# A two-layer decoder trunk: feed-forward chunk 11 as seven block products, row products in order of inner tiles, and convolution taps one slot behind their copy

## The chip, the cores and the metric

One core of a Trainium2 chip runs the whole program. The metric is the device time of one execution in microseconds (us). The engines are named as the profile names them: PE (TensorE, matmuls; PEld is its weight load), DVE (VectorE), ACT (ScalarE), POOL (GpSimd) and SP (SyncE, which issues DMAs).

## The reference

Two layers, a dilated windowed attention (layer 0) and a gated linear recurrence (layer 1), each followed by a gated convolutional feed-forward network (FFN), with a norm before and after each part. The change is in the FFN, which runs once in each layer, on 512 tokens of 1024 features:

```python
D_FF = 3 * D_MODEL           # 3072
def causal_dwconv(x, w, b):  # three taps along the tokens
    ...
    for k in range(K):
        out = out + xp[:, k:k + S] * w[k]
    return out
def conv_ffn(x, w_up, conv_w, conv_b, w_down):
    u = causal_dwconv(x @ w_up, conv_w, conv_b)
    g, v = u[..., :D_FF], u[..., D_FF:]
    return (jax.nn.gelu(g, approximate=True) * v) @ w_down
```

## The kernel before

Every float32 product is made of three matmuls on float32r operands (`mm3`, line 411): each operand is split into a rounded high part (made by ACT, line 150) and the rest (a subtraction on DVE, line 151, the "split" below), and high*high, high*low and low*high are summed in PSUM. PE runs one instruction stream, in the order in which the Python code issues it; so do DVE and ACT.

**The up projection.** D_FF is cut into 12 chunks j of 256 columns, once for the gate half g and once for the value half v. A chunk gives two inner tiles k = 2j and 2j+1 (128 features by 512 tokens). *Plain* chunks are computed tile by tile: 8 blocks of 128 input features, 3 matmuls each, so 24 matmuls 128x512 per tile (`feat_tile`, line 624; for j = 0 in two halves of 256 tokens, `feat_tiles(..., True)`). Before the change chunks 0, 1, 2 and 11 are plain, except for two value tiles of chunk 2 that serve as fillers. Chunks 3 to 10 (`SEVEN`) are computed as *seven block products*, Strassen's scheme on 2x2 blocks: per half and chunk seven products, 12 matmuls 128x256 each (`chain`, line 1006; matmuls at line 1019). Their weight sums are made in the raw weight tiles by two accumulating DMAs on POOL (line 187) and two adds on DVE (`across`, line 211, and `lower`, line 215). The token sums T that they need are built once per layer from hT by `token_sums` (line 914), a generator that runs piece by piece beside the tiles (one piece per tick) with 24 operations on DVE and 8 on ACT; its home is the buffer of the residual x, which a DMA on POOL (line 919) first saves to DRAM.

**Cycles and slots.** One chunk half is a *cycle* of ten slots (`CYCLE`). `AT` gives the slot of each of the seven products of a cycle: 1 in slot 0, 5 in slot 1, 2 in slot 2, 6 in slot 4, 3 in slot 5, 7 in slot 8, and 4 in slot 13, which is slot 3 of the next cycle. The free slots 6, 7 and 9 hold *fillers* of six matmuls 128x512: first eight quarters of the two value tiles of chunk 2, then the row products (down projection of finished inner tiles k, output columns 0 to 511, two token tiles at a time). A slot that is in no table is skipped: nothing is issued in it.

**What is issued behind a slot.** `slot` (line 366) first issues the matmuls of its step, then what `later(n, f)` put off until n slots on, then `tick`, which pumps at most one more split of a weight block for products to come. At most 16 split halves are alive, so a new split often waits until the slot that frees its buffer has ended.

**The two outputs of a cycle.** The upper output (bank y[0]) is finished by product 3: one slot later DVE adds a stored part to it (`upper`, line 1032), and `begin` runs the convolution: ACT copies the bank into u with scale and bias (line 774), then DVE adds the two shifted taps from PSUM (line 776, two instructions). The lower output (bank y[1]) first receives product 7; one slot behind product 7, DVE adds a stored part to its right half (line 1037), and product 4, on PE, accumulates onto it. So product 4 has to wait for the add of line 1037, and everything behind product 4 on PE waits with it. One slot after `begin`, `gate` multiplies g and v on DVE (line 793) or ACT applies the gelu (line 789).

After the seven-product part, `down` (line 837) runs the other half of the output columns and, for the inner tiles in `REST`, what is missing of the first.

Of the kernel before, what the change touches and what calls it, by code (L numbers as in the profile page):

```python
# [19 lines left out]
S = 512  # L20
# [15 lines left out]
TOE_BUFS = 2  # L36
CP_PAD = 8
WARM = 5
SEVEN = range(3, 11)
LAST, TAIL, REST = 11, 16, range(18, 22)  # L40
EARLIER = (0, 1, 2, 3, 22, 23, *range(4, 18))
AT = {1: 0, 5: 1, 2: 2, 6: 4, 3: 5, 7: 8, 4: 13}
CYCLE, FREE = 10, (6, 7, 9)
EARLY = 16
QUAD = {1: 0, 5: 2, 2: 3, 6: 4, 3: 6, 7: 8, 4: 12}
APART, ROUND = 7, 44
# [38 lines left out]
def kernel(  # L85
# [107 lines left out]
    def free_slots(n):  # L193

        end = CYCLE * n
        free = [CYCLE * c + r for c in range(n) for r in FREE][2:] + [end, end + 1]
        assert not {CYCLE * c + a for c in range(n) for a in AT.values()} & set(free)
        return free

# [158 lines left out]
    def side(steps, delay=1):  # L358
        sides.append([delay, steps])
# [3 lines left out]
    def later(n, f):  # L363
        due.append([n, f])
# [400 lines left out]
    def ffn(layer, hT, post, pre):  # L765
        ca, cc = ffn_cols[layer]
        neg = cp.tile([P, 144], F32, tag="neg", name=nm("neg"))
        nc.vector.tensor_scalar(neg[:, 0:96], ca, -1.0, None, op0=ALU.mult)
        nc.vector.tensor_scalar(neg[:, 96:144], cc[:, 0:48], -1.0, None, op0=ALU.mult)

        def conv(ps, j, minus=False):
            u = gen(s="u")
            near, far, own = (neg, neg, neg[:, 96:144]) if minus else (ca, ca, cc)
            nc.scalar.activation(u, ps, AF.Identity, scale=own[:, j : j + 1], bias=cc[:, 48 + j : 49 + j])  # L774
            for d, wc in ((1, near[:, 48 + j : 49 + j]), (2, far[:, j : j + 1])):
                nc.vector.scalar_tensor_tensor(  # L776
                    u[:, d:], ps[:, : S - d], wc, u[:, d:], op0=ALU.mult, op1=ALU.add
                )
            return u

        gv, ready = {}, set()

        def begin(b, ps, j, minus=False):
            m = b % 2
            k = 2 * j + m
            u = conv(ps, 24 * (b // 2) + k, minus)
            if b < 2:
                gv[k] = u
                return lambda: nc.scalar.activation(u, u, AF.Gelu_apprx_tanh)
            g = gv[k]  # L790

            def gate():
                nc.vector.tensor_tensor(g, g, u, op=ALU.mult)
                ready.add(k)

            return gate

        def tiles(j, i, bs):
            for b in bs:
                feat_tile(i, b % 2, hT, lambda ps: begin(b, ps, j))  # L800

        def gen_load(*srcs):
            o = []

            def load():
                for src in srcs:
                    o.append(gen(s="dw"))
                    nc.sync.dma_start(o[-1].rearrange("p (k c) -> p k c", c=src.shape[-1]), src)

            return o, load  # L810

        def act(k):
            assert k in ready, k
            return gv[k]

        direct = []
        for k in EARLIER:
            w = ffn_w_down[layer][k * P : (k + 1) * P, 0:512].rearrange("(k p) c -> p k c", p=P)
            o, load = gen_load(w)
            direct.append((("rows", k), load, lambda o=o: [o[0]], 0))  # L820
            direct.append((("act", k), None, lambda k=k: [act(k)], 2))
        up["direct"] = direct
        T = []
        for j in range(SEVEN[0] - 1):
            if j:
                side(token_sums(hT, T), 0)
                tiles(j, chunk(), (0, 1))
                tiles(j, chunk(), (2, 3))
            else:
                feat_tiles(2, hT, lambda b, ps: begin(b, ps, j)(), True)  # L830
        for j in (SEVEN[0] - 1, LAST):
            tiles(j, chunk(), (0, 1))
        tiles(LAST, chunk(), (2, 3))
        prep, run = down(act, post, pre)
        return run(seven(hT, T, begin, chunk(), lambda: prep(2)))

# [77 lines left out]
    def token_sums(hT, T, first=False):  # L914

        if not first:
            assert len(sides) == 1
            d = dp.tile([P, 4, D], F32, name=nm("x_kept"))
            nc.gpsimd.dma_start(d, X[0])
            kept.append(d)  # L920
# [122 lines left out]
    def seven(hT, T, begin, last, prep):  # L1043
# [2 lines left out]
        i0, acc, ends_at = state["next"], {}, CYCLE * 2 * len(SEVEN)  # L1046

        def finish(b, ps, j, minus=False):
            later(1, begin(b, ps, j, minus))

        def ends(j, half):
            return lambda ps: finish(2 * half, ps, j), lambda ps: finish(2 * half + 1, ps, j, True)
# [10 lines left out]
        fill = []  # L1063
        for m in range(2):
            fill += quarters(last, m, hT, lambda ps, m=m: finish(2 + m, ps, SEVEN[0] - 1))
        fill += [lambda k=k, p=p: rows(k, p) for k in EARLIER for p in ((0, 1), (2, 3))]
        steps = {}
        n = 0
        for j in SEVEN:
# [544 lines left out]
    for layer in range(2):  # L1614
        if layer:
# [5 lines left out]
                    w_cols(w_in, n * 256 + (D if kind == "b" else 0))  # L1621
            for c in range(4):
                w_rows(lru_w_out[0], c * 256)
        chunks = [(j, half) for j in range(SEVEN[0]) for half in range(2)]
        chunks[-1:] = [(LAST, 0), (LAST, 1), chunks[-1]]
        for j, half in chunks + [(j, half) for j in SEVEN for half in range(2)]:
            w_cols(ffn_w_up[layer], half * D_FF + j * 256, kind="seven" if j in SEVEN else "feat")
        for half, k in [(1, k) for k in range(0, TAIL, 4)] + [(0, REST[0])] + [(1, k) for k in range(TAIL, 24, 4)]:
            rows = ffn_w_down[layer][k * P : (k + 4) * P, half * 512 : half * 512 + 512]
# [86 lines left out]
```

## Time and profile before

| | |
|---|---|
| median of 3 runs | 1420.18 us (1419.66 to 1420.43) |
| the profiled execution | 1419.78 us, of which the span from first to last instruction 1418.0 us |
| PE busy | 1407.8 us (99% of the span), 8597 instructions |
| DVE busy | 1108.9 us (78%), 2173 instructions |
| ACT busy | 782.5 us (55%), 1622 instructions |
| FFN of layer 0 | up projection, plain part about 489 to 568 us, seven-product part about 568 to 794 us, then the down projection |
| FFN of layer 1 | the same from about 1029, 1108 and 1334 us |

A row of the timeline gives start, duration, engine, line, operation, output <- inputs, shapes and count, and in square brackets how long the engine had been idle before it and whose work ended that. Rows of one line that follow each other are merged (x2, x3): the duration is then that of the group. Matmuls overlap by their pipeline, so their spacing, not their duration, tells what one costs.

### The profile page before, as it was taken

Reading aid. Unit: us, or ns where it says so; the run is one execution under the profiler, and the core shown is the slowest. Engines: PE = TensorE matmul, PEld = TensorE weight load, DVE = VectorE, ACT = ScalarE, POOL = GpSimd, SP = SyncE. Lnnn points to the kernel's source line nnn. Section 1 sums busy time; section 2 is a strip of 40 time slices with the busy share of each in tenths; the row PEclk is TensorE's granted clock in tenths of the full one; section 3 lists DMA queues with packets and bytes.
Section 4 is the critical chain, followed back from the end, with each engine's and each line's share of the span. In section 5 each row is a group of like instructions: output and inputs, shape, how many; then the busy total and the mean of one; then the engine's idle time right before and its main releaser. Section 6 shows DMA issues by size and latency. Waiting matters only on the chain.

```text
span 1418.0 us, 23252 instructions
## 1 busy us (share of the span) xinstructions
PE 1407.8 (99%) x8597; PEld 1262.2 (89%) x8597; DVE 1108.9 (78%) x2173; ACT 782.5 (55%) x1622; POOL 215.3 (15%) x336
## 2 busy tenths in 40 slices
PE   9999999999999999999999999999999999999998
PEld 7888999999998898999999889888898999999886
DVE  6676898887866988988888758769788988888843
ACT  7343565353636554666656545589454655666641
POOL 0341332131310100212120001000101211111000
PEclk9999999999999999999999999999999999999999
DMA  7653464655665453756563632432444566665411
GB/s 227 180 144 111 120 181 152 173 160 164 172 189 187 153 178 82 171 120 164 120 156 84 221 119 90 134 119 73 136 149 112 120 139 144 154 130 127 167 57 59
DMA packets 167657, 199.79 MB, mean 141 GB/s; under 512 B 10432, under 2 KB 136856, under 8 KB 167288
## 3 DMA queue, kind: packets, MB, share of 16 engines
q1 hardware_dynamic: 123064, 153.34, 33.8%
q0 software_dynamic: 43632, 43.92, 16.6%
q8 instruction: 67, 1.10, 0.3%
q10 hardware_dynamic: 848, 1.05, 0.2%
q14 instruction: 46, 0.38, 0.1%
HBM read 179.31 MB, written 18.96 MB: 140 GB/s over the span
## 4 chain that ended last, share of the span: by engine, by line
PE 77%; DVE 4%; ACT 4%; issue 1%; DVEq 0%; ACTq 0%
PE ps L1019 31%; PE acc L413 25%; PE ps L413 13%; PE v L1212 6%; DVE wlo L151 1%; DVE xb L1517 1%; PE O L1424 1%; PE S L1358 1%; ACT whi L150 1%; ACT sig L1538 1%; PE tr L503 1%; ACT sig L1557 0%; ACT a L1555 0%; ACT xhi L150 0%; ACT th L1556 0%
## 5 line engine op out<-in xcount | busy, mean ns | idle before, releaser
L151 DVE TENSOR_TENSOR wlo<-raw,whi 128x512 fp32r<-128x512 f32 x608 | 397.2, 685 | 103.6 <-ACT whi L150 101.0
L150 ACT ACTIVATE whi<-raw 128x512 fp32r<-128x512 f32 x608 | 358.8, 625 | 156.4 <-PE ps L1019 53.1
L413 PE MATMUL ps<-hT,whi 128*128 128x512 f32 (+1 forms) x1216 | 327.5, 357 | 0.0
L1019 PE MATMUL ps<-T,whi 128*128 128x256 f32 x1536 | 280.4, 282 | 1.4 <-DVE ps L1037 1.4
L1019 PEld LDWEIGHTS ps<-T,whi 128*128 128x128 f32 x1536 | 238.9, 189 | 5.6 <-DVE ps L1037 2.0
L413 PEld LDWEIGHTS ps<-hT,whi 128*128 128x128 f32 x1216 | 214.8, 189 | 31.4
L413 PE MATMUL ps<-hT,wlo 128*128 128x512 f32 (+1 forms) x608 | 216.2, 356 | 0.0
L1019 PE MATMUL ps<-T,wlo 128*128 128x256 f32 x768 | 215.0, 280 | 0.0
L1019 PE MATMUL ps<-hT,whi 128*128 128x256 f32 x1152 | 212.8, 283 | 0.0
L1019 PEld LDWEIGHTS ps<-hT,whi 128*128 128x128 f32 x1152 | 181.5, 191 | 3.2
L1019 PE MATMUL ps<-hT,wlo 128*128 128x256 f32 x576 | 162.9, 283 | 0.0
L187 POOL DMA_DIRECT2D raw<-in_ffn_w_up_dram x64 | 82.5, 1320 | 433.8 <-DVE wlo L151 356.2
L1019 PEld LDWEIGHTS ps<-T,wlo 128*128 128x128 f32 x768 | 146.0, 190 | 0.0
L413 PE MATMUL acc<-whi,ahi 128*128 128x512 f32 x352 | 137.5, 391 | 0.0
L413 PE MATMUL acc<-whi,alo 128*128 128x512 f32 x352 | 137.2, 390 | 0.2
L413 PE MATMUL acc<-wlo,ahi 128*128 128x512 f32 x352 | 137.0, 389 | 0.0
L776 DVE SCALAR_TENSOR_TENSOR u<-ps,cols,u 128x511 f32<-128x511 f32 (+1 forms) x128 | 95.8, 749 | 45.7 <-ACT u L774 43.3
L413 PEld LDWEIGHTS ps<-hT,wlo 128*128 128x128 f32 x608 | 114.9, 189 | 16.5
L774 ACT ACTIVATE u<-ps,cols 128x512 f32<-128x512 f32 x64 | 49.8, 778 | 113.6 <-DVE ps L1032 69.9
L1019 PEld LDWEIGHTS ps<-hT,wlo 128*128 128x128 f32 x576 | 110.2, 191 | 0.0
L1212 PE MATMUL v<-whi,hT 128*128 128x512 f32 x320 | 106.5, 396 | 0.0
L1028 ACT ACTIVATE part<-ps 128x256 f32<-128x256 f32 x144 | 54.3, 377 | 70.8 <-PE ps L1019 67.3
(206 smaller groups left out, 2125.4 us busy)
## 6 DMA issues: line engine op xcount, KB each, us to landing
raw<-in_ffn_w_up_dram SPq DMA_DIRECT2D x48, 1024.0 KB
raw<-in_attn_w_qkv_dram SPq DMA_DIRECT2D x67, 512.0 KB
raw<-in_ffn_w_up_dram POOLq DMA_DIRECT2D x64, 256.0 KB, 4.7
raw<-in_ffn_w_down_dram SPq DMA_DIRECT2D x14, 1024.0 KB
dw<-in_ffn_w_down_dram SPq DMA_DIRECT2D x40, 256.0 KB
raw<-in_lru_w_in_dram SPq DMA_DIRECT2D x8, 1024.0 KB
turned<-T POOLq DMA_DIRECT2D x26, 256.0 KB, 2.6
ft<-turned POOLq DMA_DIRECT2D x104, 64.0 KB, 4.6
```

Of the source, the lines that this page charges most:

```text
L150: nc.scalar.activation(hi, raw, AF.Copy)
L151: nc.vector.tensor_tensor(lo, raw, hi.bitcast(F32), op=ALU.subtract)
L187: nc.gpsimd.dma_start(to, src, accum_op=ALU.add)
L413: mm(dst, l[a], r[b], start=start and n == 0, stop=stop and n == 2)
L503: nc.tensor.transpose(ps[:, k * P : (k + 1) * P], xs[i][:, k * P : (k + 1) * P], ident)
L774: nc.scalar.activation(u, ps, AF.Identity, scale=own[:, j : j + 1], bias=cc[:, 48 + j : 49 + j])
L776: nc.vector.scalar_tensor_tensor(u[:, d:], ps[:, : S - d], wc, u[:, d:], op0=ALU.mult, op1=ALU.add)
L1019: mm(dst, W[wa][0][:, k, :], right[n](ha, k), start=n in (1, 5) and k == q == 0, stop=k == 3 and q == 2, skip_group_check=True,)
L1028: later(1, lambda: nc.scalar.activation(to, dst, AF.Copy))
L1212: mm(bank, hT[a][:, k, t * P : (t + 1) * P], W[b][k % 2][:, 0, :], start=(k, a, b) == (0, 0, 0), stop=(k, a, b) == (KD - 1, 1, 0),)
L1358: mm(ps[:, c], q[hh][:, c], k[hh][:, c], start=True, stop=True)
L1424: mm(po[:, c], vtile(v, r, 2 * gi + hh), pts[gi][:, r], start=gi == 0, stop=gi == 1)
```

## The change

- `SEVEN` becomes chunks 3 to 11: chunk 11 is no longer four plain tiles but two more cycles at the end of the seven-product part (18 cycles instead of 16 per layer). The order of the weight loads follows.
- The row products take the inner tiles 0 to 19 in order (before: 0 to 3, 22, 23, 4 to 17), and `REST` is 20 to 23 instead of 18 to 21. The number of fillers stays 48, so with two more cycles slot 9 is left out in cycles 3 to 8: these have two fillers instead of three, and nine slots.
- In the seven-product part the two taps are put off by one slot: ACT's copy is issued where it was, the taps one slot later (`later(0, taps)`). In the plain part they stay right behind the copy.
- `token_sums` starts at the fifth tick after the start of chunk 0 instead of with chunk 1.

```diff
--- before.py
+++ after.py
@@ -36,11 +36,10 @@
 TOE_BUFS = 2
 CP_PAD = 8
 WARM = 5
-SEVEN = range(3, 11)
-LAST, TAIL, REST = 11, 16, range(18, 22)
-EARLIER = (0, 1, 2, 3, 22, 23, *range(4, 18))
+SEVEN = range(3, 12)
+TAIL, REST = 16, range(20, 24)
 AT = {1: 0, 5: 1, 2: 2, 6: 4, 3: 5, 7: 8, 4: 13}
-CYCLE, FREE = 10, (6, 7, 9)
+CYCLE = 10
 EARLY = 16
 QUAD = {1: 0, 5: 2, 2: 3, 6: 4, 3: 6, 7: 8, 4: 12}
 APART, ROUND = 7, 44
@@ -193,7 +192,7 @@
     def free_slots(n):
 
         end = CYCLE * n
-        free = [CYCLE * c + r for c in range(n) for r in FREE][2:] + [end, end + 1]
+        free = [CYCLE * c + r for c in range(n) for r in ((6, 7, 9) if c < 3 or c > 8 else (6, 7))][2:] + [end, end + 1]
         assert not {CYCLE * c + a for c in range(n) for a in AT.values()} & set(free)
         return free
 
@@ -772,18 +771,25 @@
             u = gen(s="u")
             near, far, own = (neg, neg, neg[:, 96:144]) if minus else (ca, ca, cc)
             nc.scalar.activation(u, ps, AF.Identity, scale=own[:, j : j + 1], bias=cc[:, 48 + j : 49 + j])
-            for d, wc in ((1, near[:, 48 + j : 49 + j]), (2, far[:, j : j + 1])):
-                nc.vector.scalar_tensor_tensor(
-                    u[:, d:], ps[:, : S - d], wc, u[:, d:], op0=ALU.mult, op1=ALU.add
-                )
-            return u
+
+            def taps():
+                for d, wc in ((1, near[:, 48 + j : 49 + j]), (2, far[:, j : j + 1])):
+                    nc.vector.scalar_tensor_tensor(
+                        u[:, d:], ps[:, : S - d], wc, u[:, d:], op0=ALU.mult, op1=ALU.add
+                    )
+
+            return u, taps
 
         gv, ready = {}, set()
 
-        def begin(b, ps, j, minus=False):
+        def begin(b, ps, j, minus=False, apart=False):
             m = b % 2
             k = 2 * j + m
-            u = conv(ps, 24 * (b // 2) + k, minus)
+            u, taps = conv(ps, 24 * (b // 2) + k, minus)
+            if apart:
+                later(0, taps)
+            else:
+                taps()
             if b < 2:
                 gv[k] = u
                 return lambda: nc.scalar.activation(u, u, AF.Gelu_apprx_tanh)
@@ -814,23 +820,21 @@
             return gv[k]
 
         direct = []
-        for k in EARLIER:
+        for k in range(REST[0]):
             w = ffn_w_down[layer][k * P : (k + 1) * P, 0:512].rearrange("(k p) c -> p k c", p=P)
             o, load = gen_load(w)
             direct.append((("rows", k), load, lambda o=o: [o[0]], 0))
             direct.append((("act", k), None, lambda k=k: [act(k)], 2))
         up["direct"] = direct
         T = []
+        side(token_sums(hT, T), 5)
         for j in range(SEVEN[0] - 1):
             if j:
-                side(token_sums(hT, T), 0)
                 tiles(j, chunk(), (0, 1))
                 tiles(j, chunk(), (2, 3))
             else:
                 feat_tiles(2, hT, lambda b, ps: begin(b, ps, j)(), True)
-        for j in (SEVEN[0] - 1, LAST):
-            tiles(j, chunk(), (0, 1))
-        tiles(LAST, chunk(), (2, 3))
+        tiles(SEVEN[0] - 1, chunk(), (0, 1))
         prep, run = down(act, post, pre)
         return run(seven(hT, T, begin, chunk(), lambda: prep(2)))
 
@@ -914,7 +918,7 @@
     def token_sums(hT, T, first=False):
 
         if not first:
-            assert len(sides) == 1
+            assert len(sides) == 1, len(sides)
             d = dp.tile([P, 4, D], F32, name=nm("x_kept"))
             nc.gpsimd.dma_start(d, X[0])
             kept.append(d)
@@ -1046,7 +1050,7 @@
         i0, acc, ends_at = state["next"], {}, CYCLE * 2 * len(SEVEN)
 
         def finish(b, ps, j, minus=False):
-            later(1, begin(b, ps, j, minus))
+            later(1, begin(b, ps, j, minus, True))
 
         def ends(j, half):
             return lambda ps: finish(2 * half, ps, j), lambda ps: finish(2 * half + 1, ps, j, True)
@@ -1063,7 +1067,7 @@
         fill = []
         for m in range(2):
             fill += quarters(last, m, hT, lambda ps, m=m: finish(2 + m, ps, SEVEN[0] - 1))
-        fill += [lambda k=k, p=p: rows(k, p) for k in EARLIER for p in ((0, 1), (2, 3))]
+        fill += [lambda k=k, p=p: rows(k, p) for k in range(REST[0]) for p in ((0, 1), (2, 3))]
         steps = {}
         n = 0
         for j in SEVEN:
@@ -1621,9 +1625,7 @@
                     w_cols(w_in, n * 256 + (D if kind == "b" else 0))
             for c in range(4):
                 w_rows(lru_w_out[0], c * 256)
-        chunks = [(j, half) for j in range(SEVEN[0]) for half in range(2)]
-        chunks[-1:] = [(LAST, 0), (LAST, 1), chunks[-1]]
-        for j, half in chunks + [(j, half) for j in SEVEN for half in range(2)]:
+        for j, half in [(j, half) for j in range(12) for half in range(2)]:
             w_cols(ffn_w_up[layer], half * D_FF + j * 256, kind="seven" if j in SEVEN else "feat")
         for half, k in [(1, k) for k in range(0, TAIL, 4)] + [(0, REST[0])] + [(1, k) for k in range(TAIL, 24, 4)]:
             rows = ffn_w_down[layer][k * P : (k + 4) * P, half * 512 : half * 512 + 512]
```

The order of instructions shows three places (numbers behind a name tell buffers apart; line numbers of the changed kernel differ by up to 6).

The first is DVE at the end of cycle 3 in layer 0. Before, from the add of the upper output (line 1032) to the add that product 4 waits for (line 1037); u1386 is the upper output, u1391 a value tile of chunk 2 that the fillers have finished:

```order
L1032 TENSOR_TENSOR ps1374_7038<-ps1374_7038,part1370_7031 128x512
L776 SCALAR_TENSOR_TENSOR u1386_7135<-ps1374_7038,cols249_1202,u1386_7135 128x511
L776 SCALAR_TENSOR_TENSOR u1386_7135<-ps1374_7038,cols249_1202,u1386_7135 128x510
L151 TENSOR_TENSOR wlo1388_7140<-u1217_6139,whi1387_7139 128x512
L776 SCALAR_TENSOR_TENSOR u1391_7151<-ps1359_6961,cols249_1202,u1391_7151 128x511
L776 SCALAR_TENSOR_TENSOR u1391_7151<-ps1359_6961,cols249_1202,u1391_7151 128x510
L793 TENSOR_TENSOR u1360_6970<-u1360_6970,u1386_7135 128x512
L151 TENSOR_TENSOR wlo1393_7169<-raw1321_6728,whi1392_7168 128x512
L793 TENSOR_TENSOR u1264_6367<-u1264_6367,u1391_7151 128x512
L1037 TENSOR_TENSOR ps1369_7018<-ps1369_7018,part1371_7032 128x256
```

And now, from line 1036 (the same add) to line 1041 (the add that product 4 waits for); u1359 is the upper output, u1364 the value tile of chunk 2:

```order
L1036 TENSOR_TENSOR ps1347_6880<-ps1347_6880,part1343_6873 128x512
L150 TENSOR_TENSOR wlo1361_6980<-raw1313_6687,whi1360_6979 128x512
L777 SCALAR_TENSOR_TENSOR u1359_6977<-ps1347_6880,cols249_1202,u1359_6977 128x511
L777 SCALAR_TENSOR_TENSOR u1359_6977<-ps1347_6880,cols249_1202,u1359_6977 128x510
L799 TENSOR_TENSOR u1333_6812<-u1333_6812,u1359_6977 128x512
L777 SCALAR_TENSOR_TENSOR u1364_6991<-ps1332_6803,cols249_1202,u1364_6991 128x511
L777 SCALAR_TENSOR_TENSOR u1364_6991<-ps1332_6803,cols249_1202,u1364_6991 128x510
L150 TENSOR_TENSOR wlo1366_7011<-raw1313_6687,whi1365_7010 128x512
L799 TENSOR_TENSOR u1258_6374<-u1258_6374,u1364_6991 128x512
L1041 TENSOR_TENSOR ps1342_6860<-ps1342_6860,part1344_6874 128x256
```

The split that stood behind the taps of the upper output now stands ahead of them, its ACT half being issued behind the copy into u; the two gates, the second pair of taps and the other split still stand ahead of the last add.

The second is PE between product 7 (output ps1369) of cycle 3 and product 1 of cycle 4 (ps1399), before:

```order
L1019 MATMUL ps1369_7018<-T1221_6147,whi1355_6940 128x256
L1019 MATMUL ps1369_7018<-T1220_6146,wlo1356_6941 128x256
L413 MATMUL acc1394_7172<-whi1350_6904,whi1352_6920 128x512
L413 MATMUL acc1394_7172<-wlo1351_6905,whi1352_6920 128x512
L413 MATMUL acc1394_7172<-whi1350_6904,wlo1353_6921 128x512
L413 MATMUL acc1395_7176<-whi1350_6904,whi1352_6920 128x512
L413 MATMUL acc1395_7176<-wlo1351_6905,whi1352_6920 128x512
L413 MATMUL acc1395_7176<-whi1350_6904,wlo1353_6921 128x512
L1019 MATMUL ps1399_7188<-hT01043_5292,whi1345_6866 128x256
L1019 MATMUL ps1399_7188<-hT11044_5293,whi1345_6866 128x256
```

And now, product 7 into ps1342 and product 1 into ps1367:

```order
L1023 MATMUL ps1342_6860<-T1197_5994,whi1328_6780 128x256
L1023 MATMUL ps1342_6860<-T1198_5995,whi1328_6780 128x256
L1023 MATMUL ps1342_6860<-T1197_5994,wlo1329_6781 128x256
L1023 MATMUL ps1367_7014<-hT01043_5292,whi1318_6706 128x256
L1023 MATMUL ps1367_7014<-hT11044_5293,whi1318_6706 128x256
L1023 MATMUL ps1367_7014<-hT01043_5292,wlo1319_6707 128x256
```

The six matmuls of a filler that stood between the two products are gone from this place, so product 4, three products further on, comes that much sooner behind product 7.

The third is DVE in the plain part, in the last two of chunk 0's half tiles. Before, splits, taps and gates alone:

```order
L151 TENSOR_TENSOR wlo1202_6031<-raw1133_5649,whi1201_6030 128x512
L151 TENSOR_TENSOR wlo1204_6035<-raw1133_5649,whi1203_6034 128x512
L776 SCALAR_TENSOR_TENSOR u1205_6062<-ps1175_5810,cols249_1202,u1205_6062 128x511
L776 SCALAR_TENSOR_TENSOR u1205_6062<-ps1175_5810,cols249_1202,u1205_6062 128x510
L793 TENSOR_TENSOR u1194_5986<-u1194_5986,u1205_6062 128x512
L151 TENSOR_TENSOR wlo1207_6068<-raw1133_5649,whi1206_6067 128x512
L151 TENSOR_TENSOR wlo1209_6072<-raw1133_5649,whi1208_6071 128x512
L776 SCALAR_TENSOR_TENSOR u1211_6101<-ps1176_5811,cols249_1202,u1211_6101 128x511
L776 SCALAR_TENSOR_TENSOR u1211_6101<-ps1176_5811,cols249_1202,u1211_6101 128x510
L793 TENSOR_TENSOR u1200_6025<-u1200_6025,u1211_6101 128x512
```

And now, with u1217 as the first of the two tiles; B and T are the token sums:

```order
L939 TENSOR_TENSOR B1209_6039<-hT01043_5292,hT11044_5293 128x512
L939 TENSOR_TENSOR B1210_6041<-hT01043_5292,hT11044_5293 128x512
L939 TENSOR_TENSOR B1211_6043<-hT01043_5292,hT11044_5293 128x512
L939 TENSOR_TENSOR B1212_6045<-hT01043_5292,hT11044_5293 128x512
L150 TENSOR_TENSOR wlo1214_6048<-raw1133_5649,whi1213_6047 128x512
L150 TENSOR_TENSOR wlo1216_6052<-raw1133_5649,whi1215_6051 128x512
L777 SCALAR_TENSOR_TENSOR u1217_6079<-ps1175_5810,cols249_1202,u1217_6079 128x511
L777 SCALAR_TENSOR_TENSOR u1217_6079<-ps1175_5810,cols249_1202,u1217_6079 128x510
L799 TENSOR_TENSOR u1194_5986<-u1194_5986,u1217_6079 128x512
L957 TENSOR_TENSOR B1209_6039<-B1209_6039,B1211_6043 128x512
L957 TENSOR_TENSOR B1210_6041<-B1210_6041,B1212_6045 128x512
L150 TENSOR_TENSOR T1196_5993<-B1209_6039,T1196_5993 128x512
```

Four adds of the token sums stand ahead of this tile's splits and taps, and two more and two splits of T behind them; the other 16 operations of the token sums follow in the six tiles of chunks 1 and 2, behind which the cycles now begin.

## The prediction

> **What bounds the kernel now.** I read the page first, then the chain of waits in order of time, then what PE waited for.
>
> ```profile
> PE 1407.8 (99%) x8597; PEld 1262.2 (89%) x8597; DVE 1108.9 (78%) x2173; ACT 782.5 (55%) x1622; POOL 215.3 (15%) x336
> PE ps L1019 31%; PE acc L413 25%; PE ps L413 13%; PE v L1212 6%; DVE wlo L151 1%; DVE xb L1517 1%; PE O L1424 1%; PE S L1358 1%; ACT whi L150 1%; ACT sig L1538 1%; PE tr L503 1%; ACT sig L1557 0%; ACT a L1555 0%; ACT xhi L150 0%; ACT th L1556 0%
> 488.87 5.75 PE ps L413 x48
> 499.23 68.81 PE ps L413 x360
> 620.38 8.58 PE ps L1019 x72
> PE ps L1019 <- DVE ps L1037: 1.4, 2, 0.7
> ```
>
> PE is the bound, and in the FFN it has no gaps: 72 matmuls of the block products run in 8.58 us without a break. So matmuls taken away are time won, unless PE is made to wait for something else. In the whole program PE waits in the block products for one thing alone, DVE's add of line 1037, twice. One of the two is in layer 1's FFN, in cycle 2:
>
> ```profile
> 1131.76 0.40 PE L1019 MATMUL ps<-hT,whi 128*128 128x256 f32 x2
> 1150.60 0.42 DVE L1037 TENSOR_TENSOR ps<-ps,part 128x256 f32<-128x256 f32 x1
> 1151.08 0.50 PE L1019 MATMUL ps<-T,whi 128*128 128x256 f32 x2 [0.74 <-DVE ps L1037]
> ```
>
> The add ended at 1151.02 and product 4 began 0.06 us later. This handover decides the case.
>
> **The matmuls.** Two half tiles take 5.75 us, 2.875 each. The 360 matmuls from 499.23 are 5 half tiles and 10 whole ones, so a whole tile takes (68.81 - 5*2.875)/10 = 5.44 us. A product takes 8.58/6 = 1.43 us. Chunk 11 goes from 4 tiles, 21.77 us, to 14 products, 20.02 us: 1.75 us won per layer, 3.5 in the program. Fillers keep their number and their 1.38 us (rows below: 618.84 to 620.22).
>
> [...]
>
> **Product 4 and its add.** Places are counted from the start of a cycle, product 1.
>
> ```profile
> 606.09 0.40 PE L1019 MATMUL ps<-hT,whi 128*128 128x256 f32 x2
> 609.10 0.43 DVE L1037 TENSOR_TENSOR ps<-ps,part 128x256 f32<-128x256 f32 x1
> 618.84 0.40 PE L413 MATMUL acc<-whi,whi 128*128 128x512 f32 x1
> 620.22 0.40 PE L1019 MATMUL ps<-hT,whi 128*128 128x256 f32 x2
> 623.32 0.42 DVE L1037 TENSOR_TENSOR ps<-ps,part 128x256 f32<-128x256 f32 x1
> 634.36 0.40 PE L1019 MATMUL ps<-hT,whi 128*128 128x256 f32 x2
> 640.83 0.69 DVE L151 TENSOR_TENSOR wlo<-dw,whi 128x512 fp32r<-128x512 f32 x1 [0.36 <-ACT whi L150]
> 641.58 0.63 ACT L150 ACTIVATE whi<-u 128x512 fp32r<-128x512 f32 x1
> 644.75 0.69 DVE L1032 TENSOR_TENSOR ps<-ps,part 128x512 f32<-128x512 f32 x1
> 645.54 0.78 ACT L774 ACTIVATE u<-ps,cols 128x512 f32<-128x512 f32 x1 [1.32 <-DVE ps L1032]
> 646.22 0.62 ACT L150 ACTIVATE whi<-dw 128x512 fp32r<-128x512 f32 x1
> 646.35 1.53 DVE L776 SCALAR_TENSOR_TENSOR u<-ps,cols,u 128x511 f32<-128x511 f32 x2 [0.91 <-ACT u L774]
> 647.80 0.68 DVE L151 TENSOR_TENSOR wlo<-dw,whi 128x512 fp32r<-128x512 f32 x1
> 650.21 0.42 DVE L1037 TENSOR_TENSOR ps<-ps,part 128x256 f32<-128x256 f32 x1
> 652.77 0.40 PE L1019 MATMUL ps<-T,whi 128*128 128x256 f32 x2
> ```
>
> A cycle takes 14.14 us (620.22 to 634.36), and product 4 starts 4.28 us into the next one. In cycle 5 the add of the upper output (line 1032) starts 10.39 us into the cycle and the add of line 1037 at 15.85; it may start as late as 14.14 + 4.28 - 0.42 - 0.06 = 17.94. So 2.1 us are spare. Cycle 2 (add at 609.10, start 591.96) and cycle 3 (623.32, start 606.09) have the least: adds at 17.14 and 17.23.
>
> *Nine slots.* Without slot 9 the cycle takes 7*1.43 + 2*1.375 = 12.76 us, and the latest start falls to 16.56.
>
> *Taps one slot later.* They wait 0.91 us for ACT's copy today; the split that comes ahead of them now waits longer, because ACT makes its high part behind that copy: from 644.75 the copy starts 0.79 later, the high part at 1.47, ending at 2.09. So DVE goes on 2.1 us after the start of line 1032's add, where before it went on after 1.6. Back to back a DVE operation takes 0.60 us (six in 3.69 us in a row below, the last of them 0.68) and a pair of taps 1.45 (646.35 to 647.80). With split, taps, split, gate and split ahead of it the add of line 1037 comes 2.1 + 0.6 + 1.45 + 3*0.6 = 5.95 us after line 1032's, where it was 5.46: the move costs half a microsecond where it should gain nine tenths.
>
> *Where line 1032's add stands in the new cycles.* The split of slot 4 waits for its high part, and that for the PE slot that frees its buffer: the one at 641.58 starts 7.22 into the cycle and ends at 7.84. Then split 0.60, taps 1.45, split 0.60: line 1032 at 10.49, line 1037 at 16.44. That is 0.12 us within the limit of 16.56: cycles 4 to 8 just fit.
>
> *Cycle 3* does not: there a gate, the taps of chunk 2's value tile and that tile's gate stand in the way as well (the order shows them). 10.49 + 2.1 + 0.6 + 1.45 + 0.6 + 1.45 + 0.6 + 0.6 = 17.89, late by 1.33 us. Behind it everything on PE shifts, so it is paid once: 1.33 per layer, between 0 (if DVE runs half a slot sooner) and 1.9 (line 1032's add 0.6 later).
>
> **The token sums sooner.** Before, they were spread over ten tiles and DVE had rests:
>
> ```profile
> 500.67 3.69 DVE L151 TENSOR_TENSOR wlo<-raw,whi 128x512 fp32r<-128x512 f32 x6
> 511.13 1.52 DVE L776 SCALAR_TENSOR_TENSOR u<-ps,cols,u 128x511 f32<-128x511 f32 x2
> 552.58 1.53 DVE L776 SCALAR_TENSOR_TENSOR u<-ps,cols,u 128x511 f32<-128x511 f32 x2 [2.10 <-ACT u L774]
> 558.02 1.54 DVE L776 SCALAR_TENSOR_TENSOR u<-ps,cols,u 128x511 f32<-128x511 f32 x2 [2.10 <-ACT u L774]
> 567.88 0.40 PE L1019 MATMUL ps<-hT,whi 128*128 128x256 f32 x2
> 568.89 1.53 DVE L776 SCALAR_TENSOR_TENSOR u<-ps,cols,u 128x511 f32<-128x511 f32 x2 [0.29 <-ACT u L774]
> L919 POOL DMA_DIRECT2D x_kept<-x_sb x2: 559/559/559, 495.2 to 1034.9; - x2
> DMA to landing us min/median/max: 6.6/6.6/6.6
> ```
>
> The save of x is not in the way: it starts at 495.2, lands at 501.8, and by the count below the first T is written 7 us behind 512.58. DVE is the engine to look at. From 512.58, behind the taps of chunk 0's second tile (511.13 + 1.45), the new order gives it until the cycles begin 24 operations of the sums, 13 splits, 4 gates, 2 adds on weights, 43*0.60 = 25.8 us, and 8 pairs of taps, 11.6: done at 550.0. PE starts the cycles at 567.88 - 21.77 = 546.11. DVE is 3.9 us behind there, where it was 568.89 + 1.45 - 567.88 = 2.5. No plain tile waits for that: up to 16 split halves, two a tile, lie ahead. But the backlog reaches cycle 2, counting operations as above: cycle 0's line 1037 at 3.9 + 9*0.60 + 2.1 + 0.6 = 12.0 (limit: nine products and a filler less 0.48, 13.76). That is 2.05 into cycle 1; with the add itself (0.33 to the next), nine operations and two pairs of taps, line 1032 follows at 10.7 and line 1037 at 16.65. That is 2.5 into cycle 2; with the add, eleven operations and two pairs of taps, line 1032 follows at 12.35 and line 1037 at 18.3, against 17.94. The same count for today's cycle 2 gives 16.84 where the row has 17.14, so I take 0.3 more: about 0.5 us late in layer 0 (0 to 1.5). In layer 1 that place already costs 0.9 (1151.08 against 1131.76 + 18.42); I add 0.2.
>
> **Sum** against the profiled execution, 1419.78 us (0.4 under the median): -3.5, +2*1.33, +0.5, +0.2 = -0.1. So 1419.6 for an execution like that one, 1420.0 as a median. What I cost at nothing: DVE's 14 added operations per layer (6 splits, 4 adds on weights, 2 each of lines 1032 and 1037) and ACT's 12 stand in the two added cycles beside 28 us of PE; without that cover they cost up to 14*0.60 = 8.4 us per layer. POOL's 8 added DMAs stand on an engine that is busy 15%; SP issues the same loads, chunk 11's later. The order of the row products only renames operands: each inner tile is gated several cycles ahead of its filler.
>
> **Rivals.**
>
> *DVE is not late* (0.20). For it: today's cycle 3 has 0.7 us spare with the same two gates and the same second pair of taps ahead of the add, and the 0.91 us wait for ACT's copy is what the move is to fill. Then 3.5 us remain, and with layer 1's wait gone too 4.4: 1415.8 to 1416.7. Against it: losing the filler alone takes 1.38 us, twice what was spare.
>
> *The cycles with two fillers wait each time* (0.26, slower). Product 4, line 1037: with only 0.12 us spare, a DVE that is 0.4 us later in each such cycle, by one more wait for ACT of the size of the 0.36 to 0.9 us rows, makes PE wait in cycles 4 to 8 too: 10*0.3 = 3 to 10*0.5 = 5 us more, 1423 to 1425. It decides as soon as the add starts later than 16.56. Against it: DVE's work per such cycle is 13*0.60 + 2*1.45 + 0.33 + 1.5 (its wait) = 12.5 of 12.76 us, so it does not fall behind for good.
>
> *DVE becomes the bound* (0.02). If operations could not overlap, 13*0.68 + 2*1.53 + 0.42 + 1.5 = 13.8 us per cycle of 12.76 would add 1 us to each of 12 cycles: 1432. [...] Six operations of 0.68 us in 3.69 say otherwise.
>
> **How the numbers follow.** Forecast 1420.0 us, 0.52; own range 1417.4 to 1422.9. Below 0.2% (2.8 us) a measurement of this kernel cannot be told from no change. Faster by more is the first rival, 0.20; slower by more the other two, 0.28. The range 1416.4 to 1424.6 reaches into both.
>
> **What would show it.** Right: stretches of products without gaps at 1.43 us each; PE waits for line 1041 (the add's new place) once at cycle 3's product 4 in each layer, 1 to 1.6 us, and below 1 us at cycle 2's. A split instead of taps behind line 1036's add, with ACT as its releaser. DVE busy above 95% from 512 to 546 us. Wrong: no wait on line 1041 (then 1416), or one in every cycle from 3 to 8 (then 1424); a plain tile that waits for a split or a bank.

## The result and the profile after

The changed kernel took 1433.43 us (median of 4 executions, 1433.17 to 1433.46), the kernel before on the same chip 1419.92 us: a ratio of 1.0095, 95% interval 1.0077 to 1.0112. It became 13.5 us slower, where 1420.0 was forecast with a range up to 1424.6. The profiled execution took 1433.17 us, its span is 1431.3 us (before: 1418.0).

The busy line of the changed kernel's page, and its own chain of waits in order of time (start, us, what), in layer 0:

```profile
PE 1407.8 (98%) x8741; PEld 1266.5 (88%) x8741; DVE 1124.2 (79%) x2201; ACT 789.8 (55%) x1646; POOL 225.3 (16%) x344
```

```profile
489.39 5.75 PE ps L412 x48
...
628.18 10.05 PE ps L1023 x84
...
683.77 8.58 PE ps L1023 x72
...
782.70 8.58 PE ps L1023 x72
```

A product still takes 8.58/6 = 1.43 us, and from 683.77 on (cycle 10) the cycles follow each other every 14.13 us without a gap, as before. PE's busy time is what it was, 1407.8 us, although matmuls were saved; e11 below, with the same matmuls and hardly a stop, has 1404.4, so the page counts some 3 us around the stops as busy. The time lost in layer 0's products lies before cycle 10. What PE waited for in the whole program (us in total, times, longest), then PE's own waits in layer 0 by its timeline (start, length, instruction, idle before and its releaser):

```profile
PE ps L1023 <- DVE ps L1041: 10.5, 11, 1.6
...
PE ps L1023 <- ACT part L1032: 3.6, 2, 1.8
```

```profile
552.87 0.38 PE L1023 MATMUL ps<-T,whi 128*128 128x256 f32 x1 [1.78 <-ACT part L1032]
...
592.92 0.39 PE L1023 MATMUL ps<-T,whi 128*128 128x256 f32 x1 [1.60 <-DVE ps L1041]
607.30 0.51 PE L1023 MATMUL ps<-T,whi 128*128 128x256 f32 x2 [1.38 <-DVE ps L1041]
620.88 0.38 PE L1023 MATMUL ps<-T,whi 128*128 128x256 f32 x1 [0.59 <-DVE ps L1041]
647.26 0.50 PE L1023 MATMUL ps<-T,whi 128*128 128x256 f32 x2 [0.58 <-DVE ps L1041]
673.66 0.50 PE L1023 MATMUL ps<-T,whi 128*128 128x256 f32 x2 [0.58 <-DVE ps L1041]
```

Six stops per layer, at the same places in both layers. (The eleventh wait for line 1041's add in the table is not one of them: it lies at 210.85 us, ahead of the first FFN, and took 1.08 us, before 0.64.) Each costs about 0.15 us more than its row names (the start of the next matmul against the pace of 0.119 us each, 8.58/72, before it): 1.94, 1.75, 1.54 and three times 0.74, 7.45 us per layer, 14.9 in all. The first is product 6 of cycle 0, which waits for ACT's part copy of product 1; the others are product 4 of cycles 2, 3, 4, 6 and 8, which wait for DVE's add of line 1041. Together: 1418.0 - 3.5 (matmuls saved) - 0.9 (the wait of before, gone) + 14.9 = 1428.5. Of the remaining 2.8 us, 0.5 stand ahead of the first FFN, where the programs are the same (489.39 against 488.87), most of it in that wait at 210.85. Behind each of the twelve stops PE's third matmul starts 0.34 us after the first and not 0.24 (647.26 to 647.60), 1.2 in all. And at the end of each layer's cycles the last product 4 and a matmul of the down projection are late by 0.3 and 0.25 us (at 799.59 and 804.73 in layer 0), 1.1 in all.

DVE's and ACT's waits between 546 and 690 us, before (where the first 22 us of it are still plain tiles) and then after:

```profile
DVE u L776 <- ACT u L774: 12.6, 13, 2.1
...
DVE wlo L151 <- ACT whi L150: 6.3, 9, 1.1
ACT u L789 <- DVE u L776: 4.3, 6, 1.1
```

```profile
DVE wlo L150 <- ACT whi L149: 18.8, 17, 1.4
...
ACT u L795 <- DVE u L777: 17.2, 12, 2.1
ACT whi L149 <- DVE raw L210: 9.7, 11, 2.5
```

The taps no longer wait for their copy (12.6 us before), but the splits wait for their high parts instead: DVE stood 6.3 + 12.6 = 18.9 us for ACT before, and 18.8 us after. And ACT stands 17.2 us at the GELUs, for taps, where it was 4.3. That gave three theories. **ACT theory**: with the taps one slot later, the GELU, whose slot is unchanged, stands right behind them; ACT waits there, the high parts behind it are late, DVE waits for these, and line 1041's add is late. **Short-cycle theory**: a cycle of 12.76 us has no room for DVE's work, wherever the taps stand. **Backlog theory**: DVE comes late to the cycles, because four plain tiles are gone from in front of them.

### The profile page after: what moved, and what is told of

It is laid out like the page before. It is cut to its first block, busy times and chain, and to the rows that moved or that the text cites. A ratio compares the mean times of both kernels' runs of the same rounds, so it can differ in the third digit from the quotient of the medians.

```text
span 1431.3 us, 23653 instructions
## 1 busy us (share of the span) xinstructions
PE 1407.8 (98%) x8741; PEld 1266.5 (88%) x8741; DVE 1124.2 (79%) x2201; ACT 789.8 (55%) x1646; POOL 225.3 (16%) x344
## 4 chain that ended last, share of the span: by engine, by line
PE 78%; DVE 12%; ACT 6%; issue 3%; DMA 1%; POOL 0%; DVEq 0%; SPq 0%; ACTq 0%
PE ps L1023 32%; PE acc L412 24%; PE ps L412 10%; PE v L1216 7%; DVE wlo L150 3%; DVE u L777 3%; ACT whi L149 2%; PE v L1154 1%; DVE xb L1521 1%; PE O L1428 1%; PE S L1362 1%; PE S L1310 1%; DVE T L150 1%; DVE u L799 1%; DVE B L939 1%
## 5 line engine op out<-in xcount | busy, mean ns | idle before, releaser
L150 DVE TENSOR_TENSOR wlo<-raw,whi 128x512 fp32r<-128x512 f32 x620 | 410.0, 687 | 130.5 <-ACT whi L149 125.8
L1023 PE MATMUL ps<-T,whi 128*128 128x256 f32 x1664 | 305.3, 283 | 14.2 <-DVE ps L1041 10.5
L412 PE MATMUL ps<-hT,whi 128*128 128x512 f32 (+1 forms) x1088 | 288.0, 353 | 0.0
L1023 PEld LDWEIGHTS ps<-T,whi 128*128 128x128 f32 x1664 | 258.4, 189 | 21.7 <-DVE ps L1041 13.9
L1023 PE MATMUL ps<-T,wlo 128*128 128x256 f32 x832 | 232.9, 280 | 0.0
L1023 PE MATMUL ps<-hT,whi 128*128 128x256 f32 x1248 | 230.5, 283 | 0.0
L412 PE MATMUL ps<-hT,wlo 128*128 128x512 f32 (+1 forms) x544 | 191.3, 352 | 0.0
L1023 PE MATMUL ps<-hT,wlo 128*128 128x256 f32 x624 | 176.4, 283 | 0.0
L1023 PEld LDWEIGHTS ps<-T,wlo 128*128 128x128 f32 x832 | 158.1, 190 | 0.0
L777 DVE SCALAR_TENSOR_TENSOR u<-ps,cols,u 128x511 f32<-128x511 f32 x120 | 89.6, 747 | 5.0 <-ACT u L773 2.9
```

Source lines behind the costliest of these rows:

```text
L150: nc.vector.tensor_tensor(lo, raw, hi.bitcast(F32), op=ALU.subtract)
L412: mm(dst, l[a], r[b], start=start and n == 0, stop=stop and n == 2)
L777: nc.vector.scalar_tensor_tensor(u[:, d:], ps[:, : S - d], wc, u[:, d:], op0=ALU.mult, op1=ALU.add)
L1023: mm(dst, W[wa][0][:, k, :], right[n](ha, k), start=n in (1, 5) and k == q == 0, stop=k == 3 and q == 2, skip_group_check=True,)
```

## The experiments

Times are medians; "before" was measured beside each group, 1419.2 to 1419.5 us.

**e1: the taps in the slot of their copy again.**

```
-            later(1, begin(b, ps, j, minus, True))
+            later(1, begin(b, ps, j, minus))
```

> The change, but the taps again follow their copy in the same slot. Three theories. ACT theory: with the taps one slot later the GELU, which kept its slot, stands right behind them; ACT waits there (35.1 us in layer 0's cycles against 12.3 before), the high parts queued behind it are late, DVE waits for these, and the add of line 1041 with it. Then most of the 14.9 us of PE waits go: 1418 to 1422 us. Short-cycle theory: a cycle with two fillers (12.76 us) leaves DVE no time for its work, wherever the taps stand; the 0.9 us waits of the taps come back, so the waits of cycles 3 to 8 stay or grow: 1431 to 1438. Backlog theory: DVE comes to the cycles late because four plain tiles are gone from in front of them; the waits in cycles 0 and 2 (1.94 and 1.75 us per layer) stay as they are, 1430 to 1434.

1421.95 us (1420.05 to 1422.89; ratio 1.0014, interval 1.0005 to 1.0023). The ACT theory's number, and the short-cycle theory falls: the six short cycles are still there. The waits of PE in the products that the view lists:

```profile
PE ps L1023 <- ACT part L1032: 3.5, 2, 1.8
...
PE ps L1023 <- DVE ps L1041: 0.8, 1, 0.8
```

The second of them lies at 210.50 us, ahead of the first FFN. Cycle 0's stop stays in both layers, as the backlog theory had it for that place; the stop of 1.75 us in cycle 2 is gone, against that theory. Cycle 3's product 4 keeps a stop of 0.29 us per layer (at 603.83 in layer 0), which the view does not list.

**e2: taps one slot later, and the GELUs and gates one slot later with them.**

```
-            later(1, begin(b, ps, j, minus, True))
+            later(2, begin(b, ps, j, minus, True))
```

> The change, with the GELU and the gates one slot later too, so that they stand as far behind the taps as before. ACT theory: ACT's wait for line 777 falls from 35.1 us to below 20, and PE's waits of cycles 0 to 8 mostly go: 1419 to 1424 us. Short-cycle theory: the same work in the same 12.76 us, 1431 to 1434. Backlog theory: cycle 0's and cycle 2's waits stay, at best the short cycles gain: 1428 to 1434.

1425.00 us (ratio 1.0040, 1.0027 to 1.0053): 8.4 us won back, 1 us more than the ACT theory's range allowed and well below the two others'. ACT's wait for line 777 in the whole program went from 70.3 to 50.6 us, so to 25.3 per layer and not below 20; the three stops of 0.74 shrank to one of 0.33, those of cycles 2 and 3 to 0.44 and 0.81.

**e3: the short cycles spread out.**

```
-        free = [CYCLE * c + r for c in range(n) for r in ((6, 7, 9) if c < 3 or c > 8 else (6, 7))][2:] + [end, end + 1]
+        free = [CYCLE * c + r for c in range(n) for r in ((6, 7, 9) if c % 3 != 2 else (6, 7))][2:] + [end, end + 1]
```

> The change, with the six cycles of two fillers spread out: cycles 2, 5, 8, 11, 14 and 17 in place of 3 to 8. ACT theory: the waits follow the taps, not the fillers; cycles 3, 4, 6 and 7 keep a wait where DVE is behind, and 0.7 us may go per long cycle: 1426 to 1431. Short-cycle theory: every short cycle now has two long ones to recover in, so its 0.7 to 1.5 us go; only cycles 0 and 2 still wait: 1421 to 1427. Backlog theory: cycles 0, 2 and 3 keep their 5.2 us per layer, the three waits of 0.74 go: 1428 to 1430.

1439.09 us (1.0136, 1.0122 to 1.0150): missed by all three. Each short cycle waits again, 0.63 to 0.69 us in cycles 5, 8, 11 and 14 and 0.97 in cycle 17, although two long ones lie between: in cycle 5, which starts at 619.02, the add began at 636.26, 17.24 us into the cycle, where 16.56 was the limit. So it is no backlog that builds up over short cycles; the sequence inside one cycle is too long. Line 1036's add already starts at 630.34, 11.32 us into that cycle, where the prediction had 10.49; why so late, no run took apart. Some 5 us of this time are a lower clock, 0.994 to 0.995 over the whole span (last section).

**e4: the taps one slot later in the kernel before, and nothing else.** (The same edit of the taps as in the change, in the old cycles.)

> The kernel before with one part of the change alone: the taps one slot behind their copy; cycles, fillers and row products as before. ACT theory: the add of line 1037 comes later by 1 us or more in each early cycle, where 0.5 to 0.9 us were spare: PE waits 0.3 to 1 us in some four cycles of each layer, 1421 to 1426 us. Short-cycle and backlog theories: nothing is lost, and the 0.9 us wait for ACT's copy is gained: 1418.5 to 1420.5.

1424.67 us (1.0034, 1.0021 to 1.0048): this part alone costs 4 to 5 us, with all cycles at ten slots, as the ACT theory had it. PE's visible stops are fewer than it said: one of 1.71 us per layer. 2.5 us of the span's 5.0 are these (less the old one of 0.9). Another 0.8 stand ahead of the first FFN, where nothing was changed (a wait of 1.45 us at 211.12, before 0.64), and the rest in steps of PE below 0.2 us each, nearly 1 us per layer.

**e5: e1, and the GELUs of chunk 2's plain tiles behind product 1's part copy.** In the changed kernel ACT's queue at the start of cycle 0 reads:

```profile
549.89 0.63 ACT L149 ACTIVATE whi<-raw 128x512 fp32r<-128x512 f32 x1 [1.13 <-DVE raw L214]
551.40 0.63 ACT L795 ACTIVATE u<-u 128x512 f32<-128x512 f32 x1 [0.87 <-DVE u L777]
551.93 0.61 ACT L149 ACTIVATE whi<-raw 128x512 fp32r<-128x512 f32 x1
552.45 0.36 ACT L1032 ACTIVATE part<-ps 128x256 f32<-128x256 f32 x1
```

Product 1 ended near 548.1, but its part copy ran at 552.45, behind a high part that waited for a sum of weights and a GELU that waited for taps, both DVE's.

```
-        tiles(SEVEN[0] - 1, chunk(), (0, 1))
+        i = chunk()
+        for b in (0, 1):
+            feat_tile(i, b, hT, lambda ps: later(3 + b, begin(b, ps, SEVEN[0] - 1)))
```

> As e1 (taps at once), and the GELUs of chunk 2's two plain tiles are issued four and five slots into the first cycle, behind the part copy of product 1. In e1 PE still waited 1.92 us per layer in cycle 0, before product 6, for that copy on ACT (1420.1 us at a granted clock of 0.999, 1422 at 0.997 to 0.998). ACT theory: the copy is late because a GELU that waits for its taps stands ahead of it on ACT; the wait falls to 0.5 us or less per layer, 3 us less than e1: span 1415 to 1416 at a clock of 0.999, time 1417 to 1419. Backlog theory: DVE is late there, and the high part ahead of the copy waits for DVE's sums of weights anyway; the wait stays above 1.5 us: as e1.

1418.23 us (0.9991, 0.9982 to 1.0000), span 1415.8: as the ACT theory had it. The part copy in e5:

```profile
549.34 1.15 ACT L149 ACTIVATE whi<-raw 128x512 fp32r<-128x512 f32 x2 [1.73 <-DVE raw L214]
550.40 0.36 ACT L1034 ACTIVATE part<-ps 128x256 f32<-128x256 f32 x1
```

PE's stop fell from 1.92 to 0.42 us; what is left is the backlog's share, the 1.73 us that the high part waits for DVE.

**e6: the change, with ACT's copy behind the high part of its slot.**

```
+            copy = lambda: nc.scalar.activation(u, ps, AF.Identity, ...)
...
             if apart:
+                behind.append(copy)
                 later(0, taps)
...
         tick(length)
+        while behind:
+            behind.pop(0)()
```

> The change, with ACT's copy of the convolution issued behind the high part of its slot and no longer ahead of it; taps, GELU and gates as in the change. If the high part behind the copy is what costs DVE time (1.43 us behind every add of line 1036), DVE's wait for high parts falls from 144 us to below 115 and PE's waits in the short cycles (0.74 and 1.5 us) go: 1422 to 1428 us. If the GELU behind the taps is the cause, they stay: 1430 to 1434. Short-cycle theory: 1431 to 1434.

1421.76 us (1.0016, 1.0007 to 1.0026): 11.7 us won back with the taps still one slot later, slightly more than the 1422 that was the best expected. DVE's wait for high parts fell from 144.1 to 122.8 us, not below 115. PE's waits for the add, of which the 1.5 lies at 211.05, ahead of the first FFN, and the two others, 0.27 each, at product 4 of cycle 3:

```profile
PE ps L1029 <- DVE ps L1047: 2.0, 3, 1.5
```

**e7 and e8: only the GELUs, then only the gates one slot later.**

```
-            later(1, begin(b, ps, j, minus, True))
+            later(2 if b < 2 else 1, begin(b, ps, j, minus, True))
```

and, for e8,

```
+            later(1 if b < 2 else 2, begin(b, ps, j, minus, True))
```

> The change, with only the GELUs one slot later; the gates stay (e2 moved both and came to 1425.0 us). If ACT standing at the GELU is the cause, this alone gives most of e2's 8 us: 1424 to 1428. If e2 gained because a gate of DVE's moved behind the add of line 1041, nothing comes of it: 1431 to 1434.

> The change, with only the gates one slot later; the GELUs stay. ACT standing at the GELU as the cause: 1430 to 1434. The gates ahead of the add of line 1041 on DVE as the cause: 1424 to 1428.

e7: 1426.35 us (1.0048, 1.0034 to 1.0062); e8: 1433.07 us (1.0096, 1.0082 to 1.0110). So e2's gain was the GELUs'; the gates' place alone is worth nothing, though beside the GELUs' it halves cycle 3's stop (1.54 in e7, 0.81 in e2). PE's wait for the add in e7, 10.5 us in the changed kernel:

```profile
PE ps L1023 <- DVE ps L1041: 3.7, 4, 1.4
```

**e9: e5, with the end of the token sums three ticks later.**

```
         parted(2, b12)
-        yield 1 + first
+        yield 2 if first else 4
```

> As e5, and the last third of the token sums (six operations of DVE, two of ACT; first read by product 4 of cycle 0) begins three ticks later, in the first cycle. In e5 the high part ahead of the part copy still waited for DVE's sum of weights (1.73 us), and PE 0.42 us per layer. If DVE's backlog is what is left there, that wait goes: 0.6 to 0.9 us less than e5's 1418.2, with no new wait. If DVE has no room in cycles 0 and 1 either, the wait of cycle 3 (0.29 us) grows to 1 us or more: 1418.5 to 1420.5.

1423.52 us (1.0031, 1.0021 to 1.0042): a miss. PE now waits for the part copy twice in cycle 0, 1.95 and 0.82 us in layer 0. DVE's sums ran at 550.04 to 552.45 in place of 540.56 to 542.97, and ACT's high parts of them, which wait for these, moved in ahead of the part copies: the work was taken off DVE's path and put onto ACT's.

**e10: the change as it was meant, with both of ACT's orders mended (e6 and e5 together).**

> The change as it was meant (taps one slot behind their copy, six short cycles), with both of ACT's orders mended: the copy behind the high part as in e6, and the GELUs of chunk 2's plain tiles behind the part copy as in e5. ACT theory: e6's wait in cycle 0 falls from 1.92 to 0.4 us per layer and the lower clock of some executions with it: 1417.5 to 1419.5. If the taps one slot later are bad in themselves, 1420.5 to 1422.5.

1418.56 us (0.9994, 0.9985 to 1.0003). So with ACT's two orders mended the taps one slot later cost nothing, and win nothing either: e5 has 1418.23 without them.

**e11: e5, and four gates per layer out of the way.**

```
-                tiles(j, chunk(), (2, 3))
+                i = chunk()
+                for b in (2, 3):
+                    feat_tile(i, b - 2, hT, lambda ps: later(3 + b, begin(b, ps, j)))
...
-            later(1, begin(b, ps, j, minus))
+            later(3 if b > 1 and j == SEVEN[0] - 1 else 1, begin(b, ps, j, minus))
```

> As e5, with four gates per layer moved: those of chunk 1's value tiles to the end of cycle 0, and those of chunk 2's value tiles two slots later. In e5 two short waits of PE were left per layer: 0.42 us in cycle 0, where ACT's high part waits for DVE, and 0.29 us in cycle 3, where a gate stood ahead of the add of line 1037. If both are DVE's place in its own order, they go: 0.8 to 1.4 us less than e5's 1418.2, 1416.8 to 1417.4. If ACT holds the part copy for another reason, or the gates come in the way of another add, no gain: 1418 to 1419.5.

1416.16 us (0.9978, 0.9969 to 0.9987), span 1414.1: faster than both kernels. All that PE waits for the add here, in the whole program, lies at 210.53 us, ahead of the first FFN:

```profile
PE ps L1027 <- DVE ps L1045: 0.8, 1, 0.8
```

## Why the prediction was wrong

**What held.** The matmuls: e11, where PE hardly waits, has a span 3.9 us under that of before; the prediction had 3.5, and 0.9 for layer 1's old wait, together 4.4. DVE was to be over 95% busy from 512 to 546 us, and it was 33.05 of 33.50:

```profile
512.50:546.00 33.50, 33.50 (x156) 27.98 (x155) 33.05 (x52) 18.31 (x31) 3.94 (x3) 1.00 0.48 118
```

The handover named as deciding, line 1041's add against product 4, decided. The move of the taps was to lose DVE time rather than win it, which e4 and e1 show.

**What agreed by luck.** Cycle 3 was to be late by 1.33 us and PE stopped for 1.54, but the places behind that are wrong. Cycle 3 starts at 586.88; line 1036's add started 12.39 us into it (599.27) and line 1041's 19.94 (606.82), where the prediction had 10.49 and 17.89. The stop of 1.75 us that product 4 of cycle 2 makes falls into cycle 3 and moves the limit back by nearly as much, so the two hide each other. What held is the count from add to add: 7.55 us, forecast 7.40.

**The step that failed** is "line 1032 at 10.49, line 1037 at 16.44. That is 0.12 us within the limit of 16.56: cycles 4 to 8 just fit." Product 1 of cycle 6 in the changed kernel, then DVE's timeline (the add of cycle 5 first), and ACT's beside it:

```profile
629.44 0.40 PE L1023 MATMUL ps<-hT,whi 128*128 128x256 f32 x2
...
633.21 0.43 DVE L1041 TENSOR_TENSOR ps<-ps,part 128x256 f32<-128x256 f32 x1
...
637.99 1.53 DVE L777 SCALAR_TENSOR_TENSOR u<-ps,neg,u 128x511 f32<-128x511 f32 x2
639.44 0.68 DVE L150 TENSOR_TENSOR wlo<-raw,whi 128x512 fp32r<-128x512 f32 x1
640.04 0.68 DVE L799 TENSOR_TENSOR u<-u,u 128x512 f32<-128x512 f32 x1
640.64 0.69 DVE L1036 TENSOR_TENSOR ps<-ps,part 128x512 f32<-128x512 f32 x1
642.76 0.69 DVE L150 TENSOR_TENSOR wlo<-raw,whi 128x512 fp32r<-128x512 f32 x1 [1.42 <-ACT whi L149]
643.37 1.53 DVE L777 SCALAR_TENSOR_TENSOR u<-ps,cols,u 128x511 f32<-128x511 f32 x2
644.81 0.68 DVE L150 TENSOR_TENSOR wlo<-raw,whi 128x512 fp32r<-128x512 f32 x1
646.17 0.69 DVE L150 TENSOR_TENSOR wlo<-raw,whi 128x512 fp32r<-128x512 f32 x1 [0.68 <-ACT whi L149]
646.78 0.43 DVE L1041 TENSOR_TENSOR ps<-ps,part 128x256 f32<-128x256 f32 x1
```

```profile
641.43 0.78 ACT L773 ACTIVATE u<-ps,cols 128x512 f32<-128x512 f32 x1 [2.59 <-DVE ps L1036]
642.11 1.14 ACT L149 ACTIVATE whi<-raw 128x512 fp32r<-128x512 f32 x2
644.99 0.63 ACT L795 ACTIVATE u<-u 128x512 f32<-128x512 f32 x1 [1.74 <-DVE u L777]
645.53 1.13 ACT L149 ACTIVATE whi<-raw 128x512 fp32r<-128x512 f32 x2
```

Line 1036's add starts 11.20 us into the cycle and line 1041's 17.34, that is 0.78 behind the limit. The first wait, 1.42 us for the high part behind the copy, is the one the prediction had (DVE goes on 2.1 us after line 1036's add: 642.76 - 640.64 = 2.12). The second, 0.68 us, it did not have. The taps end at 644.9, so the GELU, first in ACT's queue, runs at 644.99; the high part behind it starts at 645.53 and DVE gets it at 646.17. The prediction counted what the moved taps do to DVE's queue and to the copy's, and not who waits for the taps: ACT's GELU, with high parts behind it. The gate that it counted behind line 1036's add stands ahead of it here (640.04), which moves 0.6 us from the one stretch to the other.

PE stops for 0.74 us, and only in every second cycle. Cycles 4, 6 and 8 are gate halves: a GELU waits for their taps. Cycles 5 and 7 are value halves, where a gate on DVE follows the taps and no GELU runs on ACT between the two adds. From the add of cycle 4 (620.40) to that of cycle 5 (633.21) DVE takes 12.81 us, hardly more than PE's 12.76; from there to cycle 6's (646.78) it takes 13.57. So cycles 4, 6 and 8 pay. e7 is the test: with the GELUs alone one slot later, product 1 of cycle 6 starts at 628.30, line 1036's add at 639.50 and line 1041's at 644.88. That is 11.20 and 16.58 us, so the second wait is gone and the cycle just fits, as forecast (PE loses 0.08 us).

Line 1036 to line 1041 in cycle 4 of e1, DVE and ACT, for comparison:

```profile
610.73 0.69 DVE L1036 TENSOR_TENSOR ps<-ps,part 128x512 f32<-128x512 f32 x1
612.33 1.53 DVE L777 SCALAR_TENSOR_TENSOR u<-ps,cols,u 128x511 f32<-128x511 f32 x2 [0.91 <-ACT u L773]
613.78 2.06 DVE L150 TENSOR_TENSOR wlo<-raw,whi 128x512 fp32r<-128x512 f32 x3
615.75 0.43 DVE L1041 TENSOR_TENSOR ps<-ps,part 128x256 f32<-128x256 f32 x1
```

```profile
612.20 1.14 ACT L149 ACTIVATE whi<-raw 128x512 fp32r<-128x512 f32 x2
613.96 0.64 ACT L795 ACTIVATE u<-u 128x512 f32<-128x512 f32 x1 [0.62 <-DVE u L777]
```

Here the taps wait 0.91 us, but high parts are made meanwhile and the three splits follow without a stop: 5.02 us between the two adds, against 6.14. Removing either wait is enough for a limit that is missed by 0.78: the copy's (e6) or the GELU's (e7). Both engines kept the order of issue in these rows: DVE's from 599.27 to 606.82, cycle 3, come as the order of instructions lists them, and on ACT no high part passes the GELU at 644.99, though ACT stood idle for 1.74 us before it. What fails here is two such queues that wait for each other in turn.

**Terms that were too small.** Of the 14.9 us of stops, cycle 0 makes 3.9 in both layers, cycle 2 3.5, cycle 3 3.1, and cycles 4, 6 and 8 together 4.4. Cycle 2: 0.5 us forecast, 1.75 measured; e7, with the GELUs alone moved, leaves 0.27 in layer 0, so the same GELU wait is the missing part. Cycle 0: nothing forecast ("No plain tile waits for that"), 1.94 measured; the backlog of 3.9 us was nearly right (the taps of DVE's last plain tile end at 551.2, 4.6 us behind the first product at 546.64), but it was followed only along DVE to line 1037's adds, and not across to ACT, where it holds the GELU and the high part ahead of product 1's part copy (e5). Layer 1's cycle 2 was costed at 0.2 more than its old 0.9 and stops like layer 0's.

**The rivals.** "The cycles with two fillers wait each time" came nearest: the place and the trigger were right (an add later than 16.56, by one more wait for ACT), the price of 0.3 to 0.5 us per cycle was less than the 0.74 found, and every second cycle pays. "DVE is not late" gave 1415.8 to 1416.7, and e11 lies there with 1416.16, but e11 is another kernel: its taps stand with their copy again and some GELUs and gates stand later. "DVE becomes the bound" is out: e1 has the same work on DVE in the same short cycles.

Still open: why the wait at 210 us, ahead of anything that was changed, differs from run to run (0.62 to 1.81 us in these traces), and what makes line 1036's add late in e3's short cycles.

## What to carry to other kernels

When an operation is moved later, list who waits for its result on other engines and what is queued behind each of those; two queues that were worked off in order and waited for each other in turn lengthened the path from add to add here from 5.02 to 6.14 us (cycle 4 of e1, cycle 6 of the changed kernel). Moving a wait's victim does not remove the wait: put something that is ready ahead of the waiting instruction in the queue (here the high part ahead of the copy). And where the spare is smaller than one operation, do not count on an average cycle: take the worst order of operations that occurs in any cycle.

## What the runs showed of the hardware

In some executions a stop of PE cost more than its own length: behind stops of 1.76, 2.26 and 2.96 us in e3 the granted clock fell, to as low as 0.63, 0.50 and 0.55 in windows of 3 us. Columns of these rows: stretch, its length, busy time of PE, PEld, DVE, ACT and POOL, granted clock, DMA share, GB/s. First e3, then the changed kernel, which stopped at the same places:

```profile
552.00:555.00 3.00, 2.41 (x12) 2.41 (x13) 2.73 (x5) 2.37 (x6) 0.00 (x0) 0.63 0.98 120
555.00:558.00 3.00, 3.00 (x22) 3.00 (x22) 2.43 (x5) 0.90 (x2) 1.27 (x1) 0.80 0.74 229
...
594.00:597.00 3.00, 3.00 (x16) 3.00 (x15) 2.15 (x4) 1.59 (x4) 1.30 (x1) 0.50 1.05 344
```

```profile
552.00:555.00 3.00, 2.13 (x18) 2.13 (x19) 2.73 (x5) 2.98 (x8) 0.00 (x0) 1.00 1.12 137
...
594.00:597.00 3.00, 3.00 (x28) 3.00 (x27) 2.28 (x5) 2.25 (x5) 1.11 (x1) 1.00 1.05 356
```

In e3 PE had waited 1.76 and 2.26 us just before. In the 3 us with a clock of 0.50 its matmuls 128x256 followed each other every 0.213 us (three from 594.03 to 594.67), not every 0.119. The first dip is worth 3*(0.37 + 0.20) = 1.7 us, an estimate from the clocks of its two windows, and the second as much (0.96 and 0.98 in the windows on either side). With a third, 0.88 and 0.55 behind 2.96 us in cycle 2 of layer 1, that explains 5 us of its time. The changed kernel, after 1.78 and 1.60 us, kept 1.00 in its profiled execution; its three others have mean clocks of 0.997 to 0.998 and are at most 0.3 us longer, so there a lower clock cost next to nothing. e1's eleven executions fall into three at 1420.05 to 1420.14 us with a mean clock of 0.999 and eight at 1421.57 to 1422.89 with 0.996 to 0.998; in e5, where cycle 0's stop is 0.42 us instead of 1.92, ten of eleven have 0.999. So eight of e1's eleven executions took 1.4 to 2.8 us more than the other three, at the lower clock; that the stop of nearly 2 us brings it on is likely, since behind 0.42 us one execution of eleven has 0.998 and none less.
